# First block's eight transposes in one go, two weight sums moved from POOL's DMA to VectorE, and ff2's products 2 ahead of products 5

## The chip, the cores and the metric

The kernel runs on one core of one Trainium2 chip, in float32 (split into pairs of reduced operands, below). The metric is the device time of one execution in microseconds (us); a time stands for the median of several runs. In the views PE is TensorE, DVE is VectorE, ACT is ScalarE, POOL is GpSimd and SP is SyncE; PEld is the weight load of TensorE.

## The reference

One layer of a streaming encoder over 512 frames of width 1024:

```python
u = rms_norm(h, g_mix[i])
z = u @ w_in[i]
q_a, k_a, v_a, q_b, k_b, v_b, f_b, gate_logits = jnp.split(z, SPLIT_POINTS, axis=-1)
...   # y_a: sliding window attention, y_b: forgetting attention, each projected
mixed = gates[:, :, 0] * y_a + gates[:, :, 1] * y_b
h = h + mixed @ w_mix_out[i]
u = rms_norm(h, g_mlp[i])
h = h + jnp.square(jax.nn.relu(u @ w_ff1[i])) @ w_ff2[i]
ple_gate = jax.nn.sigmoid(rms_norm(h, g_ple[i]) @ w_ple_gate[i])
h = h + ple_gate * (p[i] @ w_ple_proj[i])
```

The MLP has 4096 hidden columns; a last rms_norm follows.

## The kernel before

**Splits.** A float32 product is made of three matmuls. Each operand is split into a high part, which ScalarE casts, and a low part, which VectorE subtracts; PE then adds high x high, high x low and low x high. For activations that is hi_lo (L70 the cast, L71 the subtraction), for the weights emit_split (L324 and L325; tiles u60h, u60l and so on, numbered in the order in which the products use them, with four buffers each), for v's weights split_v (L453, L454). So every product needs both engines ahead of it.

**First block.** The 512 frames are four blocks of 128. For block 0 scale1 (L447) makes the normalized rows n_xn, PE transposes them in two halves of four 128x128 tiles (to_uT, L379, tile n_tr), hi_lo splits each half, and v_mm (L467, tiles va and vb) multiplies by v's weights, one k of eight at a time: k = 0 to 3 need half 0, k = 4 to 7 half 1. Meanwhile block 1 is prepared: square1 (L432 on ScalarE, L435 on VectorE), the mean and the power on POOL (rms_rstd, L359 n_ms, L362 n_rs), scale1, and transposes, which PE executes after the fifth and sixth k of block 0. ScalarE's, VectorE's and SyncE's order is that of the code in this part.

**MLP.** Both products are done by a scheme with seven instead of eight block products. The hidden columns come in eight groups of 512, two to a quarter; the names a and b (ff1, key f1) and A and B (ff2, key s2) are the two groups of a quarter, with the product's number behind it. The string STEPS is the order of the 28 products of a quarter; a loop goes over four quarters. Weights are loaded as quadrants by SyncE (L265), and products 4 to 7 need a sum of two quadrants, made in place by sum_source: by VectorE (L296) for ff2's products 5 and 7, else by a POOL DMA that accumulates (L298). The loop's step n emits, in this order: what becomes of the product before (win_out or s2_out, ff1_lo, ff2_op), the splits of the weights up to those of step n + 2 (advance), the sums up to those of step n + 3, the rest of ff1's activation (ff1_act, relu and square, L1263 and L1264), and the matmuls of step n.

In ff1 win_out copies some products out of PSUM (L921) and adds others to them (L925); PE's next product into the same bank waits for that. In ff2 the operand of a product comes from ff2_op: product 5 from z (a difference, L1276), 6 from u, 7 from r. h_add (L1065, L1067) adds finished tiles to h. In the views the operands of ff2 are all named o, the PSUM tiles of quarter 0 are s_0x, s_0y, s_0z, those of quarter 1 s_2x and so on. In the splits of quarter 0 before the change u69 belongs to A2, u70 to A5, u71 to B5, u72 to B2, u73 to A6, u74 to B6, u75 to A3; in quarter 1 the same products have u97 to u103. ScalarE's and VectorE's order in the MLP is decided by a scheduler, apart from the first steps.

Of the kernel before, what the change touches and what calls it, by code (L numbers as in the profile page):

```python
# [8 lines left out]
F32 = mybir.dt.float32  # L9
# [5 lines left out]
P = 128  # L15
# [27 lines left out]


SHIFT = 48
STEPS = "a1 b1 a2 a5 b5 b2 a6 b6 a7 a3 b7 b3 A1 a4 b4 B1 A2 A5 B5 B2 A6 B6 A3 A7 B7 B3 A4 B4"
ET = mybir.EngineType


# [1 line left out]
def layer_kernel(ctx: ExitStack, tc: tile.TileContext, x, p, g_mix, w_in, b_forget, swa_sinks,  # L51
                 w_br_swa, w_br_fox, w_mix_out, g_mlp, w_ff1, w_ff2, g_ple, w_ple_gate,
                 w_ple_proj, g_final, out):
    nc = tc.nc
# [13 lines left out]
    def hi_lo(hi, lo, src):  # L68

        nc.scalar.copy(hi, src)  # L70
        nc.vector.tensor_tensor(lo, src, hi.bitcast(F32), ALU.subtract)  # L71
# [51 lines left out]
    for c2 in range(2):  # L123
        q = cols(w_in, C_QB + c2 * 256, 2, f"wqb{c2}")
        k = cols(w_in, C_KB + c2 * 256, 2, f"wkb{c2}")
# [150 lines left out]
    def sum_source(i):  # L276

        if i in sources or i >= len(order) or not isinstance(order[i][1][0], (list, dict)):  # L280
            return
        emit_dma(i)
        key, (rs, pn, _), _ = order[i]

        first = {5: 1, 6: 5, 4: 6}.get(pn)
        if (first and unit_of[key[:-1] + (first,)] >= look["n"]
                or pn == 7 and unit_of[key[:-1] + (5,)] not in sources
                or any(raws[r]["tile"] is None for r in raws_of(i))):
            return
        if pn in (1, 2, 3):  # L290
            q = quadrant(i, pn in (2, 3), pn == 3)
        else:
            q = quadrant(i, 0, pn == 7)
            other = quadrant(i, *{5: (0, 1), 7: (1, 1), 6: (1, 1), 4: (1, 0)}[pn])
            if key[0] == "s2" and pn in (5, 7):
                nc.vector.tensor_tensor(q, q, other, ALU.add)  # L296
            else:
                nc.gpsimd.dma_start(q, other, accum_op=ALU.add)  # L298
        sources[i] = q if key[0] == "s2" else q.rearrange("q k (j c) -> q k j c", c=P)
# [50 lines left out]
    ident = cp.tile([P, P], F32, name="ident")  # L350
# [19 lines left out]
                                           ALU.mult)  # L370
        return xn

    def to_uT(xn, uh, ul, tb, trp, name, tg="tr", halves=(0, 1)):

        for half in halves:
            tr = trp.tile([P, 4, P], F32, tag=tg, bufs=3, name=f"{name}_tr{half}")
            for j in range(4):
                k = half * 4 + j
                nc.tensor.transpose(tr[:, j, :], xn[:, k * P:(k + 1) * P], ident)  # L379
            sl = (slice(None), slice(half * 4, half * 4 + 4), slice(tb * P, (tb + 1) * P))  # L380
            hi_lo(uh[sl], ul[sl], tr)

    def new_uT(name):
        t = up.tile([P, 2 * KT * S + SHIFT], F32R, tag="u", bufs=1, name=name)
# [6 lines left out]
    psA = ctx.enter_context(tc.tile_pool(name="psA", bufs=2, space=PSUM))  # L391
    uh, ul = new_uT("u1")
# [17 lines left out]
    xts, wvs, xn1 = [], [], {}  # L410
# [18 lines left out]
    def square1(tb):  # L429
        acc = sm.tile([P, 2], F32, tag="acc1", name=f"acc1_{tb}")  # L430
        xn = xn1[tb] = s0.tile([P, D], F32, tag="xn", bufs=2, name=f"n1_{tb}_xn")
        nc.scalar.activation(xn[:, 0:512], xts[tb][:, 0:512], AF.Square, scale=1.0 / 32,  # L432
                             accum_out=acc[:, 0:1])
        if tb < 2:
            nc.vector.tensor_tensor_reduce(out=xn[:, 512:], in0=xts[tb][:, 512:],  # L435
                                           in1=xts[tb][:, 512:], scale=1.0 / D, scalar=0.0,
                                           op0=ALU.mult, op1=ALU.add, accum_out=acc[:, 1:2])
        else:
            nc.scalar.activation(xn[:, 512:], xts[tb][:, 512:], AF.Square, scale=1.0 / 32,
                                 accum_out=acc[:, 1:2])  # L440
        return acc

    def scale1(tb, acc):
        rs = rms_rstd(acc, f"n1_{tb}")
        for half in range(2):
            sl = slice(half * 512, half * 512 + 512)
            nc.vector.scalar_tensor_tensor(xn1[tb][:, sl], xts[tb][:, sl], rs,  # L447
                                           gps[half] if tb < 2 else g_bc[:, sl],
                                           ALU.mult, ALU.mult)

    def split_v(k):
        src = wvs[k // 2][:, k % 2]
        nc.scalar.copy(wv_h[:, k], src)  # L453
        nc.vector.tensor_tensor(wv_l[:, k], src, wv_h[:, k].bitcast(F32), ALU.subtract)  # L454
# [22 lines left out]
    with tc.manual_schedule(engines={ET.Activation, ET.DVE, ET.SP}):  # L477
        load_x(0)
        load_wv(0)
        load_wv(2)  # L480
        load_x(1)
        load_wv(4)
        load_wv(6)
        load_x(2)
        load_x(3)
        bcast_row(bf_bc, b_forget[0])
        bcast_row(sink_bc, swa_sinks[0])


        warm = psA.tile([P, 4, P], F32, tag="tr", bufs=3, name="warm")  # L490

        def warm_up(n):
            for j in range(n):
                nc.tensor.transpose(warm[:, j % 4, :], ident, ident)
        warm_up(N_WARM[0])
        ps = psA.tile([P, KT], F32, tag="mm", bufs=2, name="g_colps")
        nc.tensor.transpose(ps, g_row, ident[0:KT, 0:KT])
        nc.vector.tensor_copy(g_col, ps)
        warm_up(N_WARM[1])
        gps = []  # L500
        for half in range(2):
            ps = psA.tile([P, S], F32, tag="sc", bufs=3, name=f"g_ps{half}")
            for j in range(4):
                k = half * 4 + j
                nc.tensor.transpose(ps[:, j * P:(j + 1) * P],
                                    g_col[:, k:k + 1].to_broadcast([P, P]), ident)
            gps.append(ps)
        warm_up(N_WARM[2])
        scale1(0, square1(0))
        split_v(0)  # L510
        to_uT(xn1[0], uh, ul, 0, psA, "n1_0", halves=(0,))
        v_mm(0, 0)
        for k in (1, 2, 3):
            split_v(k)
            if k == 1:
                v_mm(0, 1)
        to_uT(xn1[0], uh, ul, 0, psA, "n1_0", halves=(1,))
        v_mm(0, 2)
        v_mm(0, 3)
        acc = square1(1)  # L520
        split_v(4)
        split_v(5)
        scale1(1, acc)
        v_mm(0, 4)
        v_mm(0, 5)
        split_v(6)
        split_v(7)
        for half in range(2):
            nc.scalar.copy(g_bc[:, half * 512:half * 512 + 512], gps[half])
        to_uT(xn1[1], uh, ul, 1, psA, "n1_1")  # L530
        v_mm(0, 6)
        v_mm(0, 7)
        for tb in range(1, NT):
            if tb < NT - 1:
                acc = square1(tb + 1)
                scale1(tb + 1, acc)
            v_out(tb - 1)
            for k in range(KT):
                v_mm(tb, k)
                if k == 4 and tb < NT - 1:  # L540
                    to_uT(xn1[tb + 1], uh, ul, tb + 1, psA, f"n1_{tb + 1}")
            if tb == 2:
                unit("ka")
        v_out(NT - 1)
# [889 lines left out]
    with tc.manual_schedule(engines={ET.Activation, ET.DVE}):  # L1434
# [12 lines left out]
        acc = acc4[LT]  # L1447
# [45 lines left out]
```

## Time and profile before

| | |
|---|---|
| time, median of 3 runs | 721.35 us (721.29 to 721.5) |
| profiled execution | 721.84 us, of which the span 720.1 us |
| PE busy | 705.6 us, 98% of the span |
| VectorE, ScalarE, POOL busy | 531.5, 449.4, 87.6 us |
| mean granted clock of TensorE | 0.997 |

The span is the time between the first and the last instruction of the profiled execution. The times in the views are counted from its start. An idle time in brackets is that of the engine just before the row, with what ended it.

### The profile page before, as it was taken

Reading aid. Unit: us, or ns where it says so; the run is one execution under the profiler, and the core shown is the slowest. Engines: PE = TensorE matmul, PEld = TensorE weight load, DVE = VectorE, ACT = ScalarE, POOL = GpSimd, SP = SyncE. Lnnn points to the kernel's source line nnn. Section 1 sums busy time; section 2 is a strip of 40 time slices with the busy share of each in tenths; the row PEclk is TensorE's granted clock in tenths of the full one; section 3 lists DMA queues with packets and bytes.
Section 4 is the critical chain, followed back from the end, with each engine's and each line's share of the span. In section 5 each row is a group of like instructions: output and inputs, shape, how many; then the busy total and the mean of one; then the engine's idle time right before and its main releaser. Section 6 shows DMA issues by size and latency. Waiting matters only on the chain.

```text
span 720.1 us, 11455 instructions
## 1 busy us (share of the span) xinstructions
PE 705.6 (98%) x4229; PEld 626.6 (87%) x4229; DVE 531.5 (74%) x900; ACT 449.4 (62%) x836; POOL 87.6 (12%) x127
## 2 busy tenths in 40 slices
PE   7999999999999999999999999999999999999995
PEld 6988888888888998888899789988999889988884
DVE  5567888877696556545879985899679966997564
ACT  5547888779863553344777646874578546866452
POOL 1011211100001200002410102010300020010101
PEclk9999999999999999999999999999999999999998
DMA  9256456670364894450995598739994689079002
GB/s 290 65 155 159 109 136 154 150 197 1 118 206 116 152 339 162 160 173 11 252 220 202 105 285 168 235 87 254 190 259 113 157 234 227 31 147 349 1 30 87
DMA packets 74055, 116.72 MB, mean 162 GB/s; under 512 B 6664, under 2 KB 44048, under 8 KB 74000
## 3 DMA queue, kind: packets, MB, share of 16 engines
q1 hardware_dynamic: 65792, 86.38, 37.9%
q0 software_dynamic: 8064, 29.36, 22.2%
q8 instruction: 33, 0.54, 0.3%
q10 hardware_dynamic: 144, 0.26, 0.1%
q14 instruction: 22, 0.18, 0.1%
HBM read 72.93 MB, written 4.19 MB: 107 GB/s over the span
## 4 chain that ended last, share of the span: by engine, by line
PE 85%; DVE 9%; ACT 2%; issue 2%; DMA 1%; POOL 0%; POOLq 0%; DVEq 0%; ACTq 0%
PE pf L74 5%; PE pf L76 5%; PE pf L75 5%; PE s_6x L1309 3%; PE s_4x L1309 3%; PE s_0x L1309 3%; PE s_2x L1309 3%; PE h_sc L752 2%; PE h_pv L822 2%; PE h_tr L810 2%; PE psy L75 2%; PE psy L76 2%; PE psy L74 2%; PE psm L76 2%; PE psm L75 2%; PE psm L74 2%
## 5 line engine op out<-in xcount | busy, mean ns | idle before, releaser
L298 POOL DMA_DIRECT2D wq<-wq x26 | 23.6, 942 | 174.9 <-DVE u154l L325 25.9
L770 ACT ACTIVATE s<-s,h_nm 128x128 f32<-128x128 f32 (+1 forms) x64 | 32.6, 512 | 5.9 <-DVE h_nm L763 5.1
L359 POOL TENSOR_SCALAR n_ms<-acc 128x1 f32<-128x1 f32 x15 | 6.3, 419 | 164.8 <-ACT junk L1075 100.4
L71 DVE TENSOR_TENSOR h_ptl<-h_tr,h_pth 128x512 fp32r<-128x512 f32 (+2 forms) x40 | 22.9, 604 | 3.9 <-ACT h_pth L70 3.6
L467 PE MATMUL va<-wv_h,u 128*128 128x320 f32 x64 | 20.1, 319 | 0.8 <-ACT u L70 0.7
L70 ACT CAST h_pth<-h_tr 128x512 fp32r<-128x512 f32 (+2 forms) x40 | 19.4, 523 | 1.8 <-PE h_tr L810 1.4
L70 ACT CAST u<-n_tr 128x512 fp32r<-128x512 f32 x22 | 12.2, 586 | 13.1 <-PE n_tr L1123 5.9
L810 PE MATMUL h_tr<-ident,s 128*128 128x128 f32 x136 | 19.6, 277 | 0.2
L467 PE MATMUL vb<-wv_h,u 128*128 128x328 f32 x64 | 19.6, 313 | 0.0
L298 POOL DMA_DIRECT2D wgw<-wgw x8 | 7.1, 970 | 101.9 <-DVE u25l L325 77.7
L71 DVE TENSOR_TENSOR u<-n_tr,u 128x512 fp32r<-128x512 f32 x22 | 14.6, 685 | 6.5 <-ACT u L70 6.5
L1075 ACT ACTIVATE junk<-h_sb 128x512 f32<-128x512 f32 x16 | 10.1, 630 | 12.3 <-DVE h_sb L1065 9.8
L822 PE MATMUL h_pv<-h_pth,v 128*128 128x256 f32 (+1 forms) x64 | 17.3, 291 | 0.0
L822 PE MATMUL h_pv<-h_ptl,v 128*128 128x256 f32 (+1 forms) x64 | 16.9, 305 | 0.3 <-DVE h_ptl L71 0.3
L810 PEld LDWEIGHTS h_tr<-ident,s 128*128 128x128 f32 x136 | 15.0, 141 | 2.0 <-ACT s L790 0.5
L1399 DVE TENSOR_TENSOR sgp<-sgp,pp 128x512 f32<-128x512 f32 (+1 forms) x9 | 5.7, 633 | 14.6 <-ACT sgp L1398 14.6
L1065 DVE TENSOR_TENSOR h_sb<-psm,h_sb 128x512 f32<-128x512 f32 x8 | 5.5, 689 | 14.3 <-PE psm L76 14.3
L790 ACT ACTIVATE s<-s,h_rec 128x128 f32<-128x128 f32 (+2 forms) x32 | 14.2, 482 | 2.3 <-DVE h_rec L784 2.3
L832 DVE TENSOR_TENSOR h_ao<-h_pv,h_ao 64x512 f32<-64x512 f32 x16 | 10.9, 681 | 6.1 <-ACT h_ao L831 5.8
L758 DVE CUSTOM_DVE_ANT_0 s<-h_sc,causal 128x128 f32<-128x128 f32 (+3 forms) x32 | 13.8, 482 | 0.3 <-PE h_sc L752 0.3
L784 DVE RECIPROCAL h_rec<-h_den 128x4 f32<-128x4 f32 x16 | 3.0, 185 | 14.5 <-ACT s L770 14.3
L822 PEld LDWEIGHTS h_pv<-h_ptl,v 128*128 128x128 f32 x64 | 12.1, 188 | 1.7 <-DVE h_ptl L71 0.8
(1607 smaller groups left out, 2773.8 us busy)
## 6 DMA issues: line engine op xcount, KB each, us to landing
wq<-in_w_ff_dram SPq DMA_DIRECT2D x45, 512.0 KB, 5.7
wq<-wq POOLq DMA_DIRECT2D x26, 512.0 KB, 5.1
wq_c<-in_w_ff_dram SPq DMA_DIRECT2D x9, 512.0 KB, 5.8
wg<-in_w_in_dram SPq DMA_DIRECT2D x4, 1024.0 KB, 5.4
wgw<-in_w_in_dram SPq DMA_DIRECT2D x8, 512.0 KB, 5.2
wgw<-wgw POOLq DMA_DIRECT2D x8, 512.0 KB, 5.8
wmix<-in_w_mix_out_dram SPq DMA_DIRECT2D x4, 1024.0 KB, 4.9
wpg<-in_w_ple_gate_dram SPq DMA_DIRECT2D x4, 1024.0 KB, 8.6
```

What stands on the lines that cost most here:

```text
L70: nc.scalar.copy(hi, src)
L71: nc.vector.tensor_tensor(lo, src, hi.bitcast(F32), ALU.subtract)
L74: nc.tensor.matmul(ps, lh, rh, start=start, stop=False)
L75: nc.tensor.matmul(ps, lh, rl, start=False, stop=False)
L76: nc.tensor.matmul(ps, ll, rh, start=False, stop=stop)
L298: nc.gpsimd.dma_start(q, other, accum_op=ALU.add)
L467: nc.tensor.matmul(ps, u[:, kk_, ts_], w[:, kk_, c0:c1], start=kk_ == 0 and n == 0, stop=kk_ == KT - 1 and n == 2)
L752: nc.tensor.matmul(ps[:, off:off + n], qs[i][z][:, qb * P:(qb + 1) * P], kk[i][z][:, k0:k0 + n], start=z == 0, stop=z == 1)
L770: nc.scalar.activation(sl, sl, AF.Exp, bias=nm[:, qb:qb + 1], accum_out=den[:, qb:qb + 1])
L810: nc.tensor.transpose(tr[:, n, :], c["s"][:, o, :], ident)
L822: nc.tensor.matmul(pv[:, q0:q0 + nq, :], V2[kb][:, c["v"], :], t[:, o:o + nq, :], start=n == 0, stop=n == 2 * NT - 1, skip_group_check=True)
L1309: nc.tensor.matmul(ps, o[:, j, ts_], w[:, j, :], start=tg != "" and j == 0 and n == 0, stop=j == 1 and n == 2, skip_group_check=True)
```

## The change

Three edits. In the first block the second half's transposes stand next to the first half's, and block 1's square and the splits stand in another order. The weight sums of ff1's group 1, products 6 and 7, are made by VectorE. In STEPS the two products 2 of ff2 stand ahead of the two products 5, in every quarter.

```diff
-STEPS = "a1 b1 a2 a5 b5 b2 a6 b6 a7 a3 b7 b3 A1 a4 b4 B1 A2 A5 B5 B2 A6 B6 A3 A7 B7 B3 A4 B4"
+STEPS = "a1 b1 a2 a5 b5 b2 a6 b6 a7 a3 b7 b3 A1 a4 b4 B1 A2 B2 A5 B5 A6 B6 A3 A7 B7 B3 A4 B4"
...
-            if key[0] == "s2" and pn in (5, 7):
+            if key[0] == "s2" and pn in (5, 7) or key in (("f1", 1, 6), ("f1", 1, 7)):
                 nc.vector.tensor_tensor(q, q, other, ALU.add)
             else:
                 nc.gpsimd.dma_start(q, other, accum_op=ALU.add)
...
-    def to_uT(xn, uh, ul, tb, trp, name, tg="tr", halves=(0, 1)):
-
-        for half in halves:
-            tr = trp.tile([P, 4, P], F32, tag=tg, bufs=3, name=f"{name}_tr{half}")
-            for j in range(4):
-                k = half * 4 + j
-                nc.tensor.transpose(tr[:, j, :], xn[:, k * P:(k + 1) * P], ident)
-            sl = (slice(None), slice(half * 4, half * 4 + 4), slice(tb * P, (tb + 1) * P))
-            hi_lo(uh[sl], ul[sl], tr)
+    def to_uT_pe(xn, trp, name, half, tg="tr"):
+
+        tr = trp.tile([P, 4, P], F32, tag=tg, bufs=3, name=f"{name}_tr{half}")
+        for j in range(4):
+            k = half * 4 + j
+            nc.tensor.transpose(tr[:, j, :], xn[:, k * P:(k + 1) * P], ident)
+        return tr
+
+    def to_uT_split(tr, uh, ul, tb, half):
+        sl = (slice(None), slice(half * 4, half * 4 + 4), slice(tb * P, (tb + 1) * P))
+        hi_lo(uh[sl], ul[sl], tr)
+
+    def to_uT(xn, uh, ul, tb, trp, name, tg="tr"):
+
+        for half in range(2):
+            to_uT_split(to_uT_pe(xn, trp, name, half, tg), uh, ul, tb, half)
...
         scale1(0, square1(0))
+        trs0 = [to_uT_pe(xn1[0], psA, "n1_0", half) for half in range(2)]
         split_v(0)
-        to_uT(xn1[0], uh, ul, 0, psA, "n1_0", halves=(0,))
+        to_uT_split(trs0[0], uh, ul, 0, 0)
+        split_v(1)
         v_mm(0, 0)
-        for k in (1, 2, 3):
-            split_v(k)
-            if k == 1:
-                v_mm(0, 1)
-        to_uT(xn1[0], uh, ul, 0, psA, "n1_0", halves=(1,))
+        v_mm(0, 1)
+        split_v(2)
+        to_uT_split(trs0[1], uh, ul, 0, 1)
+        acc = square1(1)
+        split_v(3)
         v_mm(0, 2)
         v_mm(0, 3)
-        acc = square1(1)
         split_v(4)
```

VectorE's order in the first block, before (wv_l is the low part of v's weights, two rows of it with x2; L71 with n_0_tr the split of block 0's transposes; L435 the square of block 1, L447 the scaling):

```order
L454 TENSOR_TENSOR wv_l<-wv_108,wv_h 128x648
L71 TENSOR_TENSOR u_80<-n_0_tr_177,u_80 128x4x128
L454 TENSOR_TENSOR wv_l<-wv_108,wv_h 128x648
L454 TENSOR_TENSOR wv_l<-wv_111,wv_h 128x648 x2
L71 TENSOR_TENSOR u_80<-n_0_tr_204,u_80 128x4x128
L435 ISA n_1_xn,acc_1_223<-x_114 128x512
L435 ISA acc_1_223 128x1
L454 TENSOR_TENSOR wv_l<-wv_117,wv_h 128x648 x2
L447 SCALAR_TENSOR_TENSOR n_1_xn<-x_114,n_1_rs,g_ps_152 128x512
```

And now (L461 is the former L454, L442 the former L435, L454 the former L447):

```order
L461 TENSOR_TENSOR wv_l<-wv_108,wv_h 128x648
L71 TENSOR_TENSOR u_80<-n_0_tr_175,u_80 128x4x128
L461 TENSOR_TENSOR wv_l<-wv_108,wv_h 128x648
L461 TENSOR_TENSOR wv_l<-wv_111,wv_h 128x648
L71 TENSOR_TENSOR u_80<-n_0_tr_180,u_80 128x4x128
L442 ISA n_1_xn,acc_1_209<-x_114 128x512
L442 ISA acc_1_209 128x1
L461 TENSOR_TENSOR wv_l<-wv_111,wv_h 128x648
L461 TENSOR_TENSOR wv_l<-wv_117,wv_h 128x648 x2
L454 SCALAR_TENSOR_TENSOR n_1_xn<-x_114,n_1_rs,g_ps_152 128x512
```

The split of half 1 and the square moved ahead of the split of k = 3, so that three splits of weights instead of two stand between the square and the scaling.

VectorE's order around the two sums of ff1, quarter 0, before (u57l to u61l are low parts of weights, L925 the additions of win_out, L1291 the low part of an operand):

```order
L325 TENSOR_TENSOR u57l<-wq_3517,u57h 128x1024
L325 TENSOR_TENSOR u58l<-wq_3659,u58h 128x1024
L925 TENSOR_TENSOR u_('f1', 0)_3995<-('f1', 0)y,u_('f1', 0)_3995 128x512
L325 TENSOR_TENSOR u59l<-wq_t_3495,u59h 128x1024
L1291 TENSOR_TENSOR o_0_1_4068<-u_('f1', 0)_3995,o_0_1_4068 128x512
L325 TENSOR_TENSOR u60l<-wq_3517,u60h 128x1024
L325 TENSOR_TENSOR u61l<-wq_3518,u61h 128x1024
L925 TENSOR_TENSOR u_('f1', 1)_4023<-('f1', 1)y,u_('f1', 1)_4023 128x512
```

And now (L933 is the former L925, L1299 the former L1291):

```order
L325 TENSOR_TENSOR u57l<-wq_3517,u57h 128x1024
L325 TENSOR_TENSOR u58l<-wq_3659,u58h 128x1024
L296 TENSOR_TENSOR wq_3517<-wq_3517,wq_3660 128x1024
L296 TENSOR_TENSOR wq_3518<-wq_3518,wq_3660 128x1024
L933 TENSOR_TENSOR u_('f1', 0)_3995<-('f1', 0)y,u_('f1', 0)_3995 128x512
L325 TENSOR_TENSOR u59l<-wq_t_3495,u59h 128x1024
L325 TENSOR_TENSOR u60l<-wq_3517,u60h 128x1024
L1299 TENSOR_TENSOR o_0_1_4068<-u_('f1', 0)_3995,o_0_1_4068 128x512
L325 TENSOR_TENSOR u61l<-wq_3518,u61h 128x1024
L933 TENSOR_TENSOR u_('f1', 1)_4023<-('f1', 1)y,u_('f1', 1)_4023 128x512
```

Two additions L296 came in behind u58l; u60l moved ahead of the operand's low part.

ScalarE's order in ff2 of quarter 0, before (u71h is B5's weights, u72h B2's, u73h A6's; o_1_5 is the operand of B5, o_1_6 that of B6, z and u what they are cast from):

```order
L324 CAST u71h<-wq_c_4102 128x1024
L70 CAST o_0_5_4455<-z_('f1', 0)_4095 128x512
L1263 ACTIVATE r_4427<-('f1', 1)x 128x512
L1264 ACTIVATE r_4427<-r_4427 128x512
L324 CAST u72h<-wq_3659 128x1024
L70 CAST o_06_4460<-u_('f1', 0)_3995 128x512
L324 CAST u73h<-wq_3660 128x1024
L70 CAST o_1_5_4486<-z_('f1', 1)_4130 128x512
L324 CAST u74h<-wq_c_4102 128x1024
L70 CAST o_1_6_4491<-u_('f1', 1)_4023 128x512
```

And now (u71h is A5's weights, u72h B5's, u73h A6's; L1271 and L1272 are the former L1263 and L1264):

```order
L324 CAST u71h<-wq_3660 128x1024
L70 CAST o_0_5_4454<-z_('f1', 0)_4095 128x512
L1271 ACTIVATE r_4426<-('f1', 1)x 128x512
L1272 ACTIVATE r_4426<-r_4426 128x512
L324 CAST u72h<-wq_c_4102 128x1024
L70 CAST o_06_4459<-u_('f1', 0)_3995 128x512
L324 CAST u73h<-wq_3660 128x1024
L70 CAST o_1_5_4484<-z_('f1', 1)_4130 128x512
L70 CAST o_1_6_4489<-u_('f1', 1)_4023 128x512
L324 CAST u74h<-wq_c_4102 128x1024
```

The cast of A6's weights stands ahead of the cast of B5's operand in both; A5's and B5's weights moved one place back, and the weights of B6 moved behind the operand of B6. POOL's DMA for A6's sum (L298) is issued behind the split of A5's weights in both, u70 before and u71 now.

## Rows read from the trace of the kernel before

**Rows 1.** The page, section 1 (busy us, share of the span, instructions) and the first line of section 4 (shares of the chain that ended last).

```profile
PE 705.6 (98%) x4229; PEld 626.6 (87%) x4229; DVE 531.5 (74%) x900; ACT 449.4 (62%) x836; POOL 87.6 (12%) x127
PE 85%; DVE 9%; ACT 2%; issue 2%; DMA 1%; POOL 0%; POOLq 0%; DVEq 0%; ACTq 0%
```

**Rows 2.** Windows of the span: from:to, its length, then busy time (and instructions) of PE, PEld, DVE, ACT and POOL, the granted clock, DMA's share, GB/s.

```profile
7.66:16.93 9.27, 7.55 (x44) 6.21 (x45) 7.98 (x13) 6.76 (x13) 2.01 (x2) 1.00 1.08 343
16.93:85.00 68.07, 68.04 (x406) 61.71 (x407) 45.74 (x145) 43.46 (x128) 10.49 (x19) 1.00 0.48 131
...
483.00:560.00 77.00, 76.86 (x505) 69.91 (x504) 63.34 (x75) 48.99 (x65) 10.39 (x12) 1.00 0.78 192
```

**Rows 3.** The waits of PE: who waits for whom, us in total, times, longest.

```profile
PE n_tr L379 <- DVE n_xn L447: 1.1, 2, 0.6
PE s_0z L1309 <- DVE o L71: 0.7, 1, 0.7
PE ('f1', 0)x L910 <- ACT u_('f1', 0)_4203 L921: 0.7, 1, 0.7
```

**Rows 4.** The timeline of the first block: start, us, engine, line and operation, and in brackets the idle time before it with its releaser.

```profile
8.99 0.41 PE L467 MATMUL va<-wv_h,u 128*128 128x320 f32 x1 [0.68 <-ACT u L70]
9.60 2.32 DVE L454 TENSOR_TENSOR wv_l<-wv,wv_h 128x648 fp32r<-128x648 f32 x3
...
12.45 0.69 DVE L71 TENSOR_TENSOR u<-n_tr,u 128x512 fp32r<-128x512 f32 x1 [0.52 <-ACT u L70]
...
13.69 1.58 DVE L454 TENSOR_TENSOR wv_l<-wv,wv_h 128x648 fp32r<-128x648 f32 x2
...
13.91 1.44 POOL L359 TENSOR_SCALAR n_ms<-acc 128x1 f32<-128x1 f32 x1 [7.09 <-DVE acc L435]
...
16.04 1.41 DVE L447 SCALAR_TENSOR_TENSOR n_xn<-x,n_rs,g_ps 128x512 f32<-128x512 f32 x2 [0.77 <-POOL n_rs L362]
...
16.93 1.29 PE L379 MATMUL n_tr<-ident,n_xn 128*128 128x128 f32 x8 [0.60 <-DVE n_xn L447]
```

**Rows 5.** ff1, quarter 0: the line of VectorE's sums (ns min/median/max, first and last start), then the timelines of POOL, DVE, ACT and PE around the stall.

```profile
L296 DVE TENSOR_TENSOR wq<-wq,wq x4: 1216/1218/1226, 394.7 to 617.5; 128x1024 f32<-128x1024 f32 x4
...
363.02 1.76 POOL L298 DMA_DIRECT2D wq<-wq  x2 [3.80 <-DVE u57l L325]
...
363.79 0.68 DVE L925 TENSOR_TENSOR u_('f1', 0)_3995<-('f1', 0)y,u_('f1', 0)_3995 128x512 f32<-128x512 f32 x1
...
370.22 1.22 DVE L325 TENSOR_TENSOR u60l<-wq,u60h 128x1024 fp32r<-128x1024 f32 x1 [2.71 <-ACT u60h L324]
...
369.13 1.05 ACT L324 CAST u60h<-wq 128x1024 fp32r<-128x1024 f32 x1 [2.35 <-DMA wq<-wq]
...
373.21 0.63 ACT L1263 ACTIVATE u_('f1', 1)_4023<-u_('f1', 1)_4023 128x512 f32<-128x512 f32 x1 [0.65 <-DVE u_('f1', 1)_4023 L925]
...
376.02 0.58 ACT L921 COPY u_('f1', 0)_4203<-('f1', 0)x 128x512 f32<-128x512 f32 x1
...
375.70 0.28 PE L910 MATMUL ('f1', 1)x<-u,u60l 128*128 128x256 f32 x1
376.65 0.50 PE L910 MATMUL ('f1', 0)x<-at_ff,u61h 128*128 128x256 f32 x2 [0.68 <-ACT u_('f1', 0)_4203 L921]
```

**Rows 6.** ff2, quarter 1: the timelines of POOL, ACT, DVE and PE.

```profile
474.53 0.86 POOL L298 DMA_DIRECT2D wq<-wq  x1 [25.86 <-DVE u98l L325]
...
479.55 1.05 ACT L324 CAST u101h<-wq 128x1024 fp32r<-128x1024 f32 x1 [0.99 <-DMA wq<-wq]
480.50 0.61 ACT L70 CAST o<-z_('f1', 3)_4895 128x512 fp32r<-128x512 f32 x1
...
475.48 1.22 DVE L325 TENSOR_TENSOR u99l<-wq_c,u99h 128x1024 fp32r<-128x1024 f32 x1
...
481.96 0.68 DVE L71 TENSOR_TENSOR o<-z_('f1', 3)_4895,o 128x512 fp32r<-128x512 f32 x1
...
490.84 1.21 DVE L325 TENSOR_TENSOR u103l<-wq,u103h 128x1024 fp32r<-128x1024 f32 x1
...
482.16 0.39 PE L1309 MATMUL s_2z<-u99l,o 128*128 128x512 f32 x1
482.69 0.73 PE L1309 MATMUL s_2z<-u99h,o 128*128 128x512 f32 x2
...
493.50 0.39 PE L1309 MATMUL s_2z<-u103l,o 128*128 128x512 f32 x1
```

**Rows 7.** ff2, quarter 0: the timelines of POOL, ACT, DVE and PE.

```profile
397.35 0.86 POOL L298 DMA_DIRECT2D wq<-wq  x1 [24.75 <-DVE u70l L325]
...
401.93 1.05 ACT L324 CAST u73h<-wq 128x1024 fp32r<-128x1024 f32 x1 [0.56 <-DMA wq<-wq]
...
395.84 1.21 DVE L325 TENSOR_TENSOR u70l<-wq,u70h 128x1024 fp32r<-128x1024 f32 x1
...
398.30 1.22 DVE L325 TENSOR_TENSOR u71l<-wq_c,u71h 128x1024 fp32r<-128x1024 f32 x1
...
404.43 0.39 PE L1309 MATMUL s_0z<-u71l,o 128*128 128x512 f32 x1
405.51 0.73 PE L1309 MATMUL s_0z<-u71h,o 128*128 128x512 f32 x2 [0.69 <-DVE o L71]
...
416.32 0.39 PE L1309 MATMUL s_0z<-u75l,o 128*128 128x512 f32 x1
```

## The prediction

> **What bounds the kernel now.** I read the shares of the engines first, then the chain that ended last, then PE's waits, and only then the stretches around them. PE is busy 98% of the span, VectorE 74%, ScalarE 62%, and 85% of the chain that ended last is PE [rows 1]. So only time in which PE stands still can be won, and the windows say where that is: between 7.66 and 16.93 us PE is busy 7.55 of 9.27 us, while from 16.93 to 85 it is busy 68.04 of 68.07 and in one quarter of the MLP (483 to 560) 76.86 of 77.00 [rows 2]. PE's own list of waits names the first block's n_tr (1.1 us in two waits), one matmul on a split operand (s_0z, 0.7) and one on a copy of ScalarE (f1's x, 0.7) [rows 3]. The size of a stall I take from start to start: in ff2 matmuls of 512 columns follow each other every 0.227 us, in ff1 those of 256 columns every 0.114.
>
> The first two quarters of ff2 show the same place twice. In quarter 0 the third matmul of B5 starts 1.08 us after the one before (404.43 to 405.51), 0.85 more than the step; with the restart, whose row of two is 0.73 instead of 0.62, that is 0.96 [rows 7]. In quarter 1 it is 482.16 to 482.69, 0.53 and so 0.30 too much, with the restart 0.41 [rows 6]; quarters 2 and 3 have a stall of that size at the same product (an estimate: the windows' idle time there is as small). The ff1 stall is 375.70 to 376.65, 0.95 less 0.114 = 0.84, with the restart 0.95 [rows 5].
>
> **First block.** The chain to the next transposes (16.93) goes over VectorE: the split of half 1 (12.45, after 0.52 of idle time in which it waits for ScalarE's cast), the square, two weight splits (13.69), then 0.77 of idle time until POOL's n_rs, then the scaling (16.04) [rows 4]. All eight transposes now stand before the first v product. PE waited 0.68 there for the cast of half 0 (8.99), so the four that are moved (0.6 us) are free, and half 1 is split without a wait: on VectorE behind the splits of v1 and v2, which end at 9.60 plus two pitches of 0.75, so from about 11.1 to 11.8; the square from 11.7 to 12.4. Only then comes v3's split (to 13.15), then v4's and v5's (1.57 for two) and the scaling. What decides the end is whether POOL's n_ms and n_rs are hidden behind these splits. At best POOL finds a gap of 0.15 before v4's split, that split starts at 13.3 and the scaling follows at 14.87: a gain of 1.17. At worst the splits leave POOL no turn: they end at about 14.7, then 0.77 as before, 15.45: a gain of 0.6. I take 0.8, nearer to the worse end, since the row of before shows that delay.
>
> That row is n_ms at 13.91: 1.44 us for a 128x1 operation, which ends only after the two splits of 13.69 have (15.27) [rows 4]. The Trainium skill, page "SBUF — State Buffer", section "Who interferes with whom", says that a VectorE instruction with two SBUF inputs and a GpSimd instruction that reads SBUF exclude each other for a whole instruction, and that who issues first decides. The trace agrees, with 1.44 us. By that rule alone the gain would be 0.6 and the time 0.2 later than I say; by the row's best case it would be 1.17.
>
> PE is full from there to 85 us, so what is won moves everything after it, unless a wait that is not tied to PE takes it back.
>
> **ff1, quarter 0.** Before, two sums of weights are issued by POOL together at 363.02; ScalarE's cast of the first, u60h, starts only at 369.13, after 2.35 of idle time. From it hang u60l (370.22), u61l, u1's addition, the square (373.21) and the copy that PE waits for (376.02) [rows 5]. Now VectorE sums both: 2 x 1.22 us (the same operation of 128x1024 in ff2; two in a row overlap a little, 1.13 apart), behind u58l, so from 363.79 to 366.1. That time is hidden: before 370.22 VectorE idled 2.71 [rows 5]. Without that cover it would cost 2.3 us of VectorE, not of PE. u0's addition moves from 363.79 to 366.1, u60h is cast from about 365.0, u60l and u61l are done by 371.4, u1's addition starts about 371.3 to 372.0, its square at the latest at 372.05, 1.16 earlier than 373.21. The copy is then done at 375.4 to 375.5, and PE's slot is 375.81: the stall of 0.95 is gone with about 0.3 to spare.
>
> **ff2.** B2 now stands between A2 and A5, so B5 comes one product, 12 matmuls x 0.227 = 2.72 us, later, and its own wait (0.3 to 0.85) goes. But A5's split also comes one later, and it is behind this split that POOL issues the sum of A6's weights. ScalarE's order puts the cast of A6's weights (u73h, in quarter 1 u101h) ahead of the cast of B5's operand; behind that cast stand B5's split and the rest of VectorE's queue, to the weights of A3. Quarter 1 in numbers [rows 6]: A5's place in VectorE's queue is now that of u99l, which ends at 475.48 + 1.22 = 476.70; 0.30 later the sum is issued (from 397.05 to 397.35 in quarter 0 [rows 7]), at 477.0 instead of 474.53. From issue to cast it took 5.02 here (474.53 to 479.55) and 4.58 in quarter 0 (397.35 to 401.93). The cast then starts between 481.6 and 482.0, the next cast 0.95 later, 0.61 long, and VectorE splits B5's operand at 483.2 to 483.6 instead of 481.96. From the start of this split to the end of u103l VectorE had 10.09 us of work without a hole (481.96 to 490.84 + 1.21), and the order of the new program has the same instructions there: u103l ends at 493.3 to 493.7. A3's second matmul, which needs it, would stand at 493.50 - 0.41 = 493.09. So PE stalls 0.25 to 0.65 there, with the restart 0.35 to 0.75; the middle is about what B5 cost. Quarters 1 to 3 gain nothing: bounds +0.3 and -0.1 each.
>
> In quarter 0 [rows 7] u71l ends at 398.30 + 1.22 = 399.52, the sum goes out at 399.82, the cast starts at 404.4 to 404.85, the split at 406.05 to 406.5, and 10.09 later A3's weights are there: 416.15 to 416.6. The slot is 416.32 - 0.96 = 415.36. That is a stall of 0.8 to 1.25, but VectorE ran back to back and 0.5 later against PE than in quarter 1, a remainder of the late ff1; without it 0.3 to 0.75. Against 0.96 I take a gain of 0.3 (bounds 0.7 and -0.3).
>
> **Sum.** 0.8 + 0.95 + 0.3 + 0 = 2.05 us. The profiled execution is 721.84, so 719.8 by it; the median of the runs is 0.49 lower, 721.35, and 719.3 by that. From no change this kernel's times tell about 0.2%, 1.44 us.
>
> **Rivals.**
> - *A, all of ff2's stalls go.* If the sum is cast under 4.3 us after its issue, A3's weights come in time. For it: in quarter 1 a second such sum, B6's, followed A6's one split later and shared the queues with it, and now the second split stands further behind the first. Against: neither row is under 4.5. Then 0.8 + 0.95 + 0.96 + 3 x 0.41 = 3.94 us go: 717.4.
> - *B, the first block gives nothing.* PE has 0.03 us of idle time from 16.93 to 85, which speaks against; a load that lands by its own time would take the gain back. 720.1.
> - *C, slower: A6's sum is late.* All of VectorE's queue up to A3 now hangs on one transfer, four times. In ff1 such a cast began 6.1 us after the issue (363.02 to 369.13, two sums together) [rows 5]. Each 0.1 us beyond my 4.8 (the middle of 4.58 and 5.02) costs 0.1 in each quarter: at 5.3 all of the gain of 2.05 is used up, at 6.1 the time is 719.3 + 4 x 1.3 = 724.5. Against: the same sum took 4.6 and 5.0.
> - *D, the ff1 chain is as late as before by another link* (its margin is 0.3): 720.3.
>
> **How the numbers follow.** My case has 0.48 (718.4 to 719.9, from the bounds of the first block and of quarter 0), A 0.20, B 0.13, D 0.08, C 0.11 (0.07 of it over 5.7 us and so beyond 722.8, the rest within 0.2%). B and D end within 0.2%. Faster 0.68, same 0.25, slower 0.07. The range from 717.3 to 720.7 holds my case, A, B and D.
>
> **What the profile of after would show.** Eight transposes ahead of the first v product and the scaling of block 1 at 14.9 to 15.5; n_ms long again if the rule holds. No PE wait at f1's product 7. In each quarter the wait for B5's operand is gone, ScalarE waits 1.5 to 2 us for a transfer before the cast of A6's weights, VectorE stands idle before it splits B5's operand, and PE waits for A3's weights. I am wrong if PE waits for A6's weights or B5's operand instead, if that cast comes over 5.2 us after its issue, or if a new wait stands between 17 and 95 us.

## The result and the profile after

The changed kernel takes 724.7 us (median of 6 runs, 723.33 to 726.1), the kernel before 721.66 beside it: a ratio of 1.0041 (95% interval 1.0031 to 1.0052). It is 0.4% slower, where 719.3 was forecast. The profiled execution has a span of 723.5 us instead of 720.1.

The shares of the engines and of the chain (the page, sections 1 and 4) answer to [rows 1]:

```profile
PE 708.3 (98%) x4229; PEld 626.6 (87%) x4229; DVE 533.9 (74%) x902; ACT 448.1 (62%) x836; POOL 85.5 (12%) x125
PE 79%; DVE 11%; DMA 4%; issue 2%; ACT 2%; SPq 0%; POOLq 0%; DVEq 0%; POOL 0%; ACTq 0%
```

PE's share of the chain fell from 85% to 79%; DMA's rose from 1% to 4%. PE's waits, against [rows 3] (who waits for whom, us in total, times, longest):

```profile
PE n_tr L378 <- DVE u L71: 1.1, 1, 1.1
PE va L474 <- DVE wv_l L461: 0.6, 1, 0.6
PE s_4z L1317 <- DVE u131l L325: 0.6, 1, 0.6
PE s_4x L1317 <- DVE u129l L325: 0.6, 1, 0.6
PE s_0x L1317 <- DVE u73l L325: 0.4, 1, 0.4
...
PE s_0x L1317 <- DVE h_sb L1075: 0.2, 1, 0.2
PE s_2x L1317 <- DVE h_sb L1075: 0.2, 1, 0.2
PE s_4x L1317 <- DVE h_sb L1075: 0.2, 1, 0.2
PE s_6x L1317 <- DVE h_sb L1075: 0.2, 1, 0.2
```

All waits of before in the first block's n_tr, in ff1 and at B5's operand are gone. New ones stand at A6's weights (u73l, u129l), at A3's (u131l), at h_sb in each quarter, and at the transposes of the last stage. In the first block a wait of 0.6 us for v's weights (va) takes the place of the 0.68 for the cast of half 0 [rows 4].

The best ledger is the start of the same matmul in the two traces; what changes from one row to the next was won or lost between them:

| matmul | before | after | lead |
|---|---|---|---|
| end of the first block (first with u0h) | 43.01 | 41.83 | -1.18 |
| ff1, quarter 0, product 7 (first with u61l) | 376.99 | 374.81 | -2.18 |
| A6, quarter 0 (first with u73h) | 410.63 | 407.45 | -3.18 |
| B7, quarter 0 (u77h) | 421.54 | 419.99 | -1.55 |
| A6, quarter 1 (u101h) | 487.81 | 485.83 | -1.98 |
| B7, quarter 1 (u105h) | 498.72 | 497.78 | -0.94 |
| A6, quarter 2 (u129h) | 565.00 | 563.85 | -1.14 |
| B7, quarter 2 (u133h) | 575.90 | 577.01 | +1.11 |
| A6, quarter 3 (u157h) | 642.22 | 642.85 | +0.63 |
| B7, quarter 3 (u161h) | 653.13 | 654.97 | +1.84 |
| last stage, weights u169h | 689.37 | 692.89 | +3.52 |

Up to A6 of the first quarter everything came as forecast or better: 3.18 us ahead. Then every quarter loses 1.0 to 2.3 us between A6 and B7, where the three quarters behind the first win only 0.4 to 0.5 at B5; quarter 2 loses another 0.24 in ff1, and the last stage loses 1.7. By the starts of the matmuls in between, with the restarts, the four quarters lose 1.8 us at A6's weights (0.7 and 0.8 of it in quarters 0 and 2), 2.2 at A3's and 2.0 at A7's bank, some 0.5 in each quarter.

Where a quarter loses is seen in its queues. Quarter 1, POOL, ACT, DVE and PE in this order (start, us, instruction, idle time before it), against [rows 6]:

```profile
475.44 0.86 POOL L298 DMA_DIRECT2D wq<-wq  x1 [28.02 <-DVE u99l L325]
480.51 0.86 POOL L298 DMA_DIRECT2D wq_c<-wq  x1 [4.21 <-DVE r L1287]
...
480.17 1.05 ACT L324 CAST u101h<-wq 128x1024 fp32r<-128x1024 f32 x1 [3.17 <-DMA wq<-wq]
485.10 1.06 ACT L324 CAST u102h<-wq_c 128x1024 fp32r<-128x1024 f32 x1 [1.39 <-DMA wq_c<-wq]
...
481.77 0.69 DVE L71 TENSOR_TENSOR o<-z_('f1', 3)_4895,o 128x512 fp32r<-128x512 f32 x1 [1.28 <-ACT o L70]
490.65 1.22 DVE L325 TENSOR_TENSOR u103l<-wq,u103h 128x1024 fp32r<-128x1024 f32 x1
494.13 1.29 DVE L1075 SCALAR_TENSOR_TENSOR h_sb<-s_2x,h_sb 128x512 f32<-128x512 f32 x2
...
491.41 0.39 PE L1317 MATMUL s_2z<-u103h,o 128*128 128x512 f32 x1
491.93 0.50 PE L1317 MATMUL s_2z<-u103l,o 128*128 128x512 f32 x1
...
494.33 0.39 PE L1317 MATMUL s_2z<-u103h,o 128*128 128x512 f32 x1
494.96 0.47 PE L1317 MATMUL s_2x<-u104h,o 128*128 128x512 f32 x1 [0.24 <-DVE h_sb L1075]
495.27 0.40 PE L1317 MATMUL s_2x<-u104l,o 128*128 128x512 f32 x1
```

A6's sum goes out at 475.44 and is cast 4.73 us later, after ScalarE waited 3.17 us for it. VectorE then splits B5's operand at 481.77, 1.28 us late, and 10.10 us later the low part of A3's weights is done (490.65 + 1.22): the prediction's chain with its own length. PE waits 0.29 there. But the queue goes on to the h_add of product 6 (494.13), and product 7 writes the bank which that h_add reads: PE starts it 0.41 us late (494.96, where 0.63 instead of 0.22 passed since the row before). B6's sum, too, goes out 5.07 us behind A6's; it was 2.70 before.

A6's weights stand in the same queue, ahead of A3's. In quarter 0, where VectorE split B5's operand 1.85 us late, PE waits for them:

```profile
408.24 0.50 PE L1317 MATMUL s_0x<-u73l,o 128*128 128x512 f32 x1 [0.40 <-DVE u73l L325]
```

### The profile page after: what moved, and what is told of

Read it like the earlier page. It is cut to its first block, busy times and chain, and to the rows that moved or that the text cites. A ratio compares the mean times of both kernels' runs of the same rounds, so it can differ in the third digit from the quotient of the medians.

```text
span 723.5 us, 11452 instructions
## 1 busy us (share of the span) xinstructions
PE 708.3 (98%) x4229; PEld 626.6 (87%) x4229; DVE 533.9 (74%) x902; ACT 448.1 (62%) x836; POOL 85.5 (12%) x125
## 4 chain that ended last, share of the span: by engine, by line
PE 79%; DVE 11%; DMA 4%; issue 2%; ACT 2%; SPq 0%; POOLq 0%; DVEq 0%; POOL 0%; ACTq 0%
PE pf L74 5%; PE pf L76 5%; PE pf L75 5%; PE h_sc L760 2%; PE h_pv L830 2%; PE h_tr L818 2%; PE psm L76 2%; DMA wq<-wq 2%; PE psm L74 2%; PE psy L74 2%; PE psy L76 2%; PE psm L75 2%; PE psy L75 2%; PE s_0x L1317 2%; PE s_2x L1317 2%
## 5 line engine op out<-in xcount | busy, mean ns | idle before, releaser
L298 POOL DMA_DIRECT2D wq<-wq x25 | 22.4, 947 | 179.4 <-DVE u155l L325 28.2
L71 DVE TENSOR_TENSOR h_ptl<-h_tr,h_pth 128x512 fp32r<-128x512 f32 (+2 forms) x40 | 22.9, 604 | 4.0 <-ACT h_pth L70 3.6
L298 POOL DMA_DIRECT2D wgw<-wgw x8 | 7.1, 970 | 102.1 <-DVE u25l L325 77.7
L71 DVE TENSOR_TENSOR u<-n_tr,u 128x512 fp32r<-128x512 f32 x22 | 14.6, 684 | 5.9 <-ACT u L70 5.9
```

## The experiments

**The edits taken apart.** Four kernels with one part each, or without one.

The order of ff2 undone:

```diff
-STEPS = "... B1 A2 B2 A5 B5 A6 ..."
+STEPS = "... B1 A2 A5 B5 B2 A6 ..."
```

> The changed kernel with the old order of ff2's products (A2 A5 B5 B2); the first block and the two sums by VectorE stay. Theory: all of the loss comes from the order of ff2's products, by way of the late sum of A6's weights; the two other edits keep what the trace shows of them (1.2 and 0.95 us by the lead of the matmuls at 43 and 376 us). So 721.66 - 2.15 = 719.5 us, with waits of PE for B5's operand as before (0.3 to 0.9 each). Rival 1: the two sums by VectorE and the load places that they change are the cause of late loads, in the third quarter and ahead of the last stage; then about 1.7 us of delay at the last stage stay, and the time is 721 or more.

Measured: 719.04 us, ratio 0.9968 (0.9956 to 0.9981). PE is 2.24 us ahead in ff1 and 2.8 from the first quarter of ff2 to the end. The two other edits give what their rows promised; rival 1 falls.

The new order of ff2 alone, in the kernel before:

```diff
-STEPS = "... B1 A2 A5 B5 B2 A6 ..."
+STEPS = "... B1 A2 B2 A5 B5 A6 ..."
```

> The kernel before with the new order of ff2's products alone. Theory: 724.7 + 2.15 = 726.8 us (726 to 728): PE waits in every quarter for A3's weights and for the bank of A7 (1.1 us instead of 0.4), more in the third quarter, and the last stage's first weights land 3 us later. Rival 1: the loss needs the sums by VectorE; then 722 to 723.

Measured: 727.66 us, ratio 1.0083 (1.0069 to 1.0096), within what was expected: some 6 us lost, by the same waits (PE's for h_sb in all quarters, 1.2 us at the last stage's transposes). So the loss is the order's alone.

The first block alone, all else as before:

```diff
+        trs0 = [to_uT_pe(xn1[0], psA, "n1_0", half) for half in range(2)]
...
+        to_uT_split(trs0[1], uh, ul, 0, 1)
+        acc = square1(1)
+        split_v(3)
```

> The kernel before with the first block's edit alone. Theory: PE is full from 17 to 85 us and later waits are tied to PE, so the lead of 1.2 us seen at 43 us stays to the end: 721.4 - 1.2 = 720.2 us. Rival: loads that land by their own time take it back by the MLP: 721.2 us.

Measured: 720.03 us, ratio 0.9981 (0.9972 to 0.9990), 1.2 us by the medians. The lead lasts.

The two sums alone:

```diff
-            if key[0] == "s2" and pn in (5, 7):
+            if key[0] == "s2" and pn in (5, 7) or key in (("f1", 1, 6), ("f1", 1, 7)):
```

> The kernel before with the two sums by VectorE alone. Theory: PE's wait of 0.95 us in ff1 goes, and half a microsecond of B5's wait in the first quarter, where VectorE ran late: 721.4 - 1.3 = 720.1 us. Rival: the wait moves to the next product: 721.4 us.

Measured: 720.33 us, ratio 0.9985 (0.9976 to 0.9993): 0.9 us by the medians, nearer to the 0.95 of ff1 alone than to 1.3. In the profiled executions PE's lead is 1.04 us at ff1's product 7 and 1.58 from B5 on, but the one of the kernel before is itself 0.6 us above that kernel's median (721.84 against 721.26). In the kernel with the first block's edit alone, which keeps the late sums, PE waits 0.30 us at B5 in the first quarter (403.77) and not 0.85. So the half microsecond more at this place is not shown to come from the late sums.

**Is it the late sum of A6?** The prediction's mechanism says so. First, A5 in front of B2, so that A6's sum goes out early again:

```diff
-STEPS = "... B1 A2 B2 A5 B5 A6 ..."
+STEPS = "... B1 A2 A5 B2 B5 A6 ..."
```

> The changed kernel with ff2's order A2 A5 B2 B5 instead of A2 B2 A5 B5: A5's split, behind which the sum of A6's weights goes out, is back at its old place, B5 still stands one product later. Theory: the sum goes out 2.5 us earlier against PE, ScalarE no longer waits for it ahead of the cast of B5's operand, and neither B5 nor A3 nor A7 waits: 719.5 less the four waits for B5's operand (2.2 us), 717.3 us, or up to 1.7 more if the last stage's loads stay late. Rival 2: not A6's sum but the later split of B5's weights, and with it B6's sum and the loads behind it, makes the loss; that split stays late here, so 722 to 724 us with PE's waits at A7.

Measured: 726.45 us, ratio 1.0070 (1.0057 to 1.0083). My theory fell, and rival 2 had the cause, though not the size (722 to 724 us); PE's largest waits are at A3, up to 1.7 us in the fourth quarter. In the timelines of POOL, ACT and DVE of its first quarter:

```profile
394.65 0.85 POOL L298 DMA_DIRECT2D wq<-wq  x1 [25.69 <-DVE u70l L325]
402.17 0.85 POOL L298 DMA_DIRECT2D wq_c<-wq  x1 [6.67 <-issue]
405.03 0.86 POOL L298 DMA_DIRECT2D wq<-wq_c  x1 [2.01 <-DVE u73l L325]
...
399.54 1.05 ACT L324 CAST u73h<-wq 128x1024 fp32r<-128x1024 f32 x1 [0.86 <-PE s_0y L1317]
406.68 1.05 ACT L324 CAST u74h<-wq_c 128x1024 fp32r<-128x1024 f32 x1 [2.66 <-DMA wq_c<-wq]
...
402.08 0.68 DVE L71 TENSOR_TENSOR o<-z_('f1', 1)_4130,o 128x512 fp32r<-128x512 f32 x1
407.76 1.23 DVE L325 TENSOR_TENSOR u74l<-wq_c,u74h 128x1024 fp32r<-128x1024 f32 x1 [0.87 <-ACT u74h L324]
```

The cast of A6's weights (u73h) waits for no transfer any more and B5's operand is split without a wait (402.08). But B6's sum goes out at 402.17, behind B5's split, and now ScalarE waits 2.66 us for it and VectorE 0.87 at u74l, with A3's and A7's work behind. The same wait, one product further on.

A6's sum by VectorE instead of the transfer:

```diff
-            if key[0] == "s2" and pn in (5, 7) or ...:
+            if key[0] == "s2" and (pn in (5, 7) or pn == 6 and key[1] % 2 == 0) or ...:
```

> The changed kernel with the sum of A6's weights made by VectorE (1.22 us in each quarter) instead of by the transfer; the order of products stays the new one. The scheduler now puts the cast of B5's operand ahead of the cast of A6's weights. Theory: the wait of ScalarE (3 to 3.7 us) and VectorE's idle time ahead of the split of B5's operand (1.1 to 1.9 us) go, VectorE has 1.13 us more work; its queue up to A7's bank is 0.2 to 0.8 us earlier, and A3's and A7's waits shrink by that: 722 to 723.5 us, with the last stage as late as now. Rival 2: as A6's sum isn't the cause and VectorE has more to do, 725 us or more.

Measured: 729.29 us, ratio 1.0117 (1.0097 to 1.0138). The theory (722 to 723.5) fell; rival 2's 725 us or more holds, but not its reason. VectorE does the sum at 400.75, ahead of B5's split, so that this split and with it B6's sum come later still:

```profile
404.93 0.85 POOL L298 DMA_DIRECT2D wq_c<-wq  x1 [35.56 <-DVE u_('f1', 1)_4023 L1288]
...
409.45 1.05 ACT L324 CAST u74h<-wq_c 128x1024 fp32r<-128x1024 f32 x1 [3.36 <-DMA wq_c<-wq]
...
400.75 1.22 DVE L296 TENSOR_TENSOR wq<-wq,wq 128x1024 f32<-128x1024 f32 x1
410.53 1.22 DVE L325 TENSOR_TENSOR u74l<-wq_c,u74h 128x1024 fp32r<-128x1024 f32 x1 [1.48 <-ACT u74h L324]
```

B6's sum stands at 404.93 instead of 402.12 in the changed kernel, and PE waits 0.8 us at B6's weights in each quarter. It fits that B6's sum counts, but it changes several things at once: VectorE's work, and the order on ScalarE and VectorE.

**Taking the transfers away.** The next kernels leave the sums out, both, or one at a time; the products then use a quadrant that is not summed. Without A6's sum alone, ScalarE's and VectorE's order in the MLP stays that of the changed kernel. Where B6's sum is out, the scheduler casts B6's weights ahead of B6's operand again, and VectorE splits one operand ahead of an addition to h.

```diff
-            else:
+            elif not (key[0] == "s2" and pn == 6):
                 nc.gpsimd.dma_start(q, other, accum_op=ALU.add)
```

> The changed kernel without the eight transfers that sum the weights of ff2's products 6 (both groups, all quarters; the products use an unsummed quadrant, so the output is not the reference's). The orders of ScalarE and of SyncE's last loads stay those of the changed kernel. Theory, after the run with A5 in front: not one sum but both are late, each goes out behind a split of product 5, and ScalarE's and VectorE's queues stand behind their casts. Without them PE waits for nothing in ff2: by the lead of the matmuls 3.2 us ahead at A6 of the first quarter plus three waits of 0.4, and the last stage still waits for its weights since they are loaded in the same order: 717.5 to 719.5 us. Rival: VectorE's order (product 2's h_add in front of B6's operand) makes the queue too long by itself; then PE still waits at A3 and A7 and the time is 722 us or more.

> The changed kernel without the sums of A6's weights alone (four transfers; output not the reference's); B6's sum stays behind B5's split, one product later than before the change. Theory of two late sums: like the run with A5 in front, where A6's sum was early: ScalarE waits for B6's sum, and PE at A3 and A7: 722.5 to 726 us. Theory of the prediction (A6's sum alone): 718 to 720 us.

> The changed kernel without the sums of B6's weights alone (four transfers; output not the reference's). Theory of two late sums: the wait for A6's sum ahead of B5's operand stays, and with it 0.3 to 0.7 us of waits of PE in each quarter: 721 to 723.5 us. Theory of the prediction: no better than the changed kernel, 724 us. If B6's sum alone is the cause: 718 to 720 us.

Measured: 718.0 us without both (ratio 0.9955, 0.994 to 0.997), 723.57 without A6's (1.0029, 1.0018 to 1.0041), 724.46 without B6's (1.0040, 1.0028 to 1.0051). Without both, PE waits for nothing in ff2 that the list names; its lead is 3.30 us at A6 of the first quarter, 3.74, 4.18 and 4.66 in the others: 0.4 us per quarter, B5's wait, is what the new order wins when nothing is late. Without one of them nearly all of the loss stays: PE's waits are at A3 (up to 1.4 us) and A7 without A6's sum, and at A6, A3 and A7 without B6's. So either late sum is enough, the two overlap, and VectorE's queue, with the two places just named exchanged, isn't too long when nothing is late.

How long such a sum takes differs by quarter. The fourth quarter with A5 in front, POOL and ACT:

```profile
637.15 0.86 POOL L298 DMA_DIRECT2D wq<-wq  x1 [6.58 <-ACT o L70]
640.10 0.86 POOL L298 DMA_DIRECT2D wq<-wq  x1 [2.08 <-DVE u157l L325]
...
643.25 1.05 ACT L324 CAST u158h<-wq 128x1024 fp32r<-128x1024 f32 x1 [4.17 <-DMA wq<-wq]
```

From issue to cast it took 6.10 us, with another sum issued 2.95 us behind it; in the first quarter of the same run 4.51 (402.17 to 406.68), with another sum issued 2.86 us behind it (405.03). So the second sum does not make the difference. Without A6's sum, too, B6's took 6.62 us in the third quarter (557.75 to 564.37). Why is open.

The control, the same sums taken out in the kernel of the first experiment, with the old order of ff2:

```diff
-            else:
+            elif not (key[0] == "s2" and pn == 6):
```

> The kernel with the old order of ff2's products and the two other edits, without the eight sums of ff2's products 6 (output not the reference's): the control. If what these transfers cost is only the waits behind their casts, B5's waits of 0.3 us go and 1.3 to 1.7 us with them: 717.4 us. If fewer transfers help all loads as such, the gain here is as large as in the changed order (5 us or more).

Measured: 718.34 us, ratio 0.9959 (0.9944 to 0.9974), 0.7 us less than with the sums. Neither forecast: the loads don't gain 5 us, but B5's waits of 0.3 us are all still there (402.76, 479.95, 557.13, 634.32). PE's lead in ff2 is the same in both (2.75 and 2.79). The difference lies behind the last computing instruction, VectorE's last row, with the sums and without:

```profile
712.68 0.42 DVE L1470 TENSOR_TENSOR o<-sgp,g_final_bc 128x256 f32<-128x256 f32 x1
```

```profile
712.74 0.42 DVE L1470 TENSOR_TENSOR o<-sgp,g_final_bc 128x256 f32<-128x256 f32 x1
```

The spans are 717.1 and 716.5 us, so 4.03 us follow the end of this row with the sums and 3.38 without. In all fourteen profiled executions this end goes with the number of accumulating transfers that POOL issues (L298): 4.2 us with 56, as in the kernel before, 4.0 with 54, 3.7 with 50 and 3.4 with 46, or 0.08 us each. What the program does there was not tried. So 0.65 us of what the kernel without both sums wins over the changed one, and 0.17 of what the two sums by VectorE win, belong to this end and to no wait of PE. What the control does show: with the old order B5 waits for VectorE's queue, not for A6's transfer.

**The last stage.** PE's wait there remained when both sums were taken away (661.78, where the lead fell from 4.66 to 3.52). In SyncE's order the changed kernel loads the second half of w_ple_gate, two blocks, ahead of the first half; before, one block of the second half stood ahead: the first cast follows the landing of the second of these four loads before (660.11) and of the third now (663.73). Places for the two halves exchanged:

```diff
-            w2 = sum(x >= last_ff for x in used[:n]) < 2
+            w2 = sum(x >= last_ff for x in used[:n]) >= 2
```

> The changed kernel with the places of the last stage's four weight loads exchanged, so that SyncE loads the first half's two blocks ahead of the second half's (in the changed kernel both blocks of the second half come first). Theory: what the last stage costs (PE's wait of 1.2 us before its first product, a lead of 1.84 that falls to 3.5) is the order of these loads; the wait goes and the time is 724.7 - 1.5 = 723.2 us, with ff2 unchanged. Rival: the loads are late because ff2's last sum holds SyncE's queue; then the wait stays and the time is 724.5 us.

Measured: 723.31 us, ratio 1.0024 (1.0014 to 1.0034), 1.4 us less than the changed kernel by the medians, 1.2 by the ratios. ScalarE's first cast of these weights, in the changed kernel, without the two sums, and with the places exchanged:

```profile
663.84 1.34 ACT L315 ACTIVATE u165h<-wpg,g_ple_t 128x512 fp32r<-128x512 f32 x2 [3.14 <-PE n_tr L378]
```

```profile
657.11 1.34 ACT L315 ACTIVATE u165h<-wpg,g_ple_t 128x512 fp32r<-128x512 f32 x2 [2.91 <-DMA wpg<-in_w_ple_gate_dram]
```

```profile
658.92 0.73 ACT L315 ACTIVATE u165h<-wpg,g_ple_t 128x512 fp32r<-128x512 f32 x1 [1.92 <-DVE h_sb L1075]
```

In the first the releaser is put down to PE's transposes, which ran just then (from 663.14); the second, with the same order of loads, names the transfer. With the exchange the cast comes 4.9 us earlier than in the changed kernel and PE has no wait at the transposes; in ff2 the losses stay.

**A version that beats both.** The control said that B5's wait is VectorE's queue. In the kernel with the old order, product 1's h_add (two instructions of 0.6 us) stands ahead of the split of B5's operand; it is emitted one step later:

```diff
-            elif done[1] % 2:
+            elif done[1] % 2 and done[2] != 1:
                 s2_out(done[1] // 2, done[2])
...
+        if n > 1 and steps[n - 2][0] == "s2" and steps[n - 2][1] % 2 and steps[n - 2][2] == 1:
+            s2_out(steps[n - 2][1] // 2, 1)
```

> The kernel with the old order of ff2's products and the two other edits, and product 1's h_add emitted one step later, so that VectorE splits B5's operand ahead of it. Theory after the control: B5's wait of 0.3 us (0.41 with the restart) is VectorE's queue and not the transfers, and it goes in all four quarters: 719.0 - 1.6 = 717.4 us. Rival: the h_add then comes too late for the bank of A6, whose first matmul waits instead: 719 us or more.

Measured: 717.46 us, ratio 0.9949 (0.9936 to 0.9961), 3.8 us less than the kernel before and 7.2 less than the changed one. VectorE and PE in its second quarter:

```profile
477.13 0.68 DVE L71 TENSOR_TENSOR o<-z_('f1', 3)_4895,o 128x512 fp32r<-128x512 f32 x1
...
478.33 0.68 DVE L1073 TENSOR_TENSOR h_sb<-s_2x,h_sb 128x512 f32<-128x512 f32 x1
...
479.14 0.39 PE L1317 MATMUL s_2z<-u99l,o 128*128 128x512 f32 x1
479.36 0.62 PE L1317 MATMUL s_2z<-u99h,o 128*128 128x512 f32 x2
```

The operand is split at 477.13 (479.17 with the h_add ahead), PE's step to B5's third matmul is 0.22 us, and its waits list names nothing in the MLP.

## Why the prediction was wrong

**First block: right, sized too low.** Scaling moved from 16.04 to 14.86, 1.18 us against the 0.8 I took; that was the best case of its bounds. The rows of VectorE and POOL, against [rows 4]:

```profile
12.50 2.44 DVE L461 TENSOR_TENSOR wv_l<-wv,wv_h 128x648 fp32r<-128x648 f32 x3
12.75 0.74 POOL L359 TENSOR_SCALAR n_ms<-acc 128x1 f32<-128x1 f32 x1 [5.93 <-DVE acc L442]
13.58 1.04 POOL L362 TENSOR_TENSOR n_rs<-n_ms,mhalf 128x1 f32<-128x1 f32 x1
14.86 1.40 DVE L454 SCALAR_TENSOR_TENSOR n_xn<-x,n_rs,g_ps 128x512 f32<-128x512 f32 x2
```

n_ms and n_rs took 0.74 and 1.04 us beside three splits, and both were done before these ended. It is the gap of my best case, though only some 0.03 us long: VectorE's first split ended at 13.33, the second began at 13.36, and n_ms ended at 13.50. In the ten profiled executions in which VectorE leaves a gap there (0.03 to 0.36 us) n_ms took 0.73 to 0.75 us. In the four in which it leaves none it took 1.43 to 1.45, the kernel before among them, and the one without A6's sum, whose first block is the new one:

```profile
12.56 1.43 POOL L359 TENSOR_SCALAR n_ms<-acc 128x1 f32<-128x1 f32 x1 [5.74 <-DVE acc L442]
15.11 1.41 DVE L454 SCALAR_TENSOR_TENSOR n_xn<-x,n_rs,g_ps 128x512 f32<-128x512 f32 x2 [0.46 <-POOL n_rs L362]
```

So one of the eleven executions with the new first block lost this turn; the edit alone gives 1.2 us by the medians. The Trainium skill's exclusion for a whole instruction (page "SBUF — State Buffer", section "Who interferes with whom") fits these rows if POOL gets its turn in the gap; my reading, that it waits to the end of the row of splits, was wrong: even here n_ms ended at 13.99, and the splits at 14.65.

**ff1: right**, to 0.05 us (a lead of 1.0 more at product 7).

**B5's own wait: right.** It went in all quarters (0.4 to 0.5 us each, 1.0 in the first). But the 0.96 for the first quarter is the row of one execution; as the kernel with the first block's edit alone shows, "a remainder of the late ff1" is not borne out.

**The new wait, rival C's place: right in its mechanism, and its transfer time too; the price was wrong.** A6's sum was cast 5.29, 4.73, 4.56 and 4.80 us after its issue in the four quarters, where I took 4.8. The 5.3 us from which rival C was to decide were not reached, though the first is over the 5.2 that I named as a sign of being wrong. The failing step is the sentence "So PE stalls 0.25 to 0.65 there, ... Quarters 1 to 3 gain nothing", and with it the terms 0.3 and 0 of the sum. In place of that gain the MLP from there on lost 4.0 us by the ledger, from -2.18 to +1.84, all but 0.24 of it in ff2. The wait at A3 was 0.28 to 0.33 in three quarters and 0.76 in quarter 2, without the restart. But I followed VectorE's queue from B5's operand to A3's weights and looked at its last item alone. Three things I left out:
- the queue's items ahead of A3's weights: A6's weights are among them, and PE waited for them in quarters 0 and 2 (0.57 and 0.73, without the restart), the other sign of being wrong that I had named; 1.8 us in all. In quarter 2 VectorE had before that been held 0.80 us by a load. Why just in these two was not tried;
- the queue's next item that PE needs, product 6's h_add, 12.4 us behind the split of B5's operand, on whose bank product 7 waits: 0.4 us and a restart in each quarter, 2.0 us in all;
- a second late sum, B6's. Its issue, too, stands behind a split that the change moves (B5's). I used its distance from A6's sum only as an argument for less traffic (rival A), and took VectorE's 10.09 us as "without a hole". The runs that take away one sum each show that either is enough for most of the loss.

**The last stage: not in the sum at all.** 1.7 us by the ledger, 1.2 to 1.4 by the exchange of places. The prediction spoke of waits between 17 and 95 us and of ff2, and went past SyncE's last loads.

Of the rivals, C names the right sign and place, with a price worked out for a later transfer that wasn't later; that its 724.5 for 6.1 us lies beside the 724.7 measured is luck. A's condition came true only with the sums taken away (718.0). B and D fell: the first block's gain lasts, and PE no longer waits at f1's product 7.

## What to carry to other kernels

When a step is put later, list all that is issued behind it on every queue: here two weight sums hung on the two splits that moved by one product, and each held an in-order queue with everything behind it. Follow a late queue past every item that PE needs, to its last reader, banks that are to be freed included, and not to one of them; and compare the order of loads into the next stage, too, which moved with the places though no line of it was touched. A wait of 0.3 us was worth removing by taking two additions out of its way, and not by moving products.

## What the runs showed of the hardware

- A sum by an accumulating transfer of 512 KB was cast 4.55 to 5.29 us after its issue (the eight of A6 and B6 in the changed kernel), and 6.10 and 6.62 us in quarters of two other runs, for a reason that is open; VectorE's addition of the same tile takes 1.22 us of the engine.
- Each accumulating transfer of POOL goes with 0.08 us between the last computing instruction and the end of the program (4.2 us with 56 of them, 3.4 with 46), with no wait of PE in between.
- A 128x1 POOL instruction beside VectorE's splits took 0.73 to 0.75 us where VectorE left a gap of 0.03 us or more between two of them (ten executions), and 1.43 to 1.45 where it left none (four).
